# LN0 and adaLN stage: no low parts on GpSimd, and some w_ada blocks multiplied as plain fp32 between and after LN0's transposes

## The chip, the cores and the metric

The kernel runs on one core of a Trainium2 chip. Its engines are named as in the profile: PE (TensorE matmul) and PEld (its weight load), DVE (VectorE), ACT (ScalarE), POOL (GpSimd) and SP (SyncE, which here only issues DMAs). The metric is the device time of one execution in microseconds (us).

## The reference, cut to what matters

One layer of an encoder trunk over 512 prompt rows and 64 sample rows of width 2048, in float32. The stage in question computes the first modulated input u and the first products with w_in:

```python
mod = (jax.nn.silu(c) @ w_ada + b_ada).reshape(B, 6, 1, D_MODEL)
sh1, sc1, g1, sh2, sc2, g2 = (mod[:, i] for i in range(6))
u = ln_plain(x) * (1 + sc1) + sh1
mix, k_new, v_new, pool_new = token_mixer(u, ...)      # begins with u @ w_in
```

`ln_plain` is a layer norm without parameters, c is one row for the prompt and one for the sample, w_ada is 2048 x 12288. Only sh1 and sc1 (columns 0 to 4095, 33.6 MB) belong to this stage; the other four are computed on DVE during attention.

## The kernel before

Matmuls are made in two or three fp32r products: a matrix is split into a high part (`hi`, an fp32r copy by ACT) and a low part (`lo`, the float32 value minus `hi`). The helper `Weights` does it for streamed weights: SP loads a block of 512 KB into a slot (L174), `advance` lets ACT write `hi` (L202) and then DVE or POOL write `lo` (L207). `take` hands PE the pair of a block and keeps three blocks split ahead. A slot is free for the next load when `lo` is written.

The stage in program order, which each engine follows strictly:

- x arrives in five tiles of 128 tokens (the last has 64). `stats` computes mean and variance on DVE and centres the tile (L496 on DVE, for tiles 1 and 3 L494 on ACT). `xpose` transposes it on PE in four groups of four (L507), one PSUM bank `AT[b]` for each group, and ACT copies the banks to axt (L512). A small product (L514) and `rs_evac` spread 1/std over the partitions.
- Then 64 w_ada blocks, in eight groups of eight: the loop at L604. A block is 512 rows of 256 columns, and four blocks make 256 columns of sh1 or sc1. `c4` holds silu(c) as high and low parts in four columns, so L613 and L614 are eight matmuls of 256 columns a block: `c4` times `hi`, `c4` times `lo`. The blocks alternate between DVE and POOL for their low part: `(None, nc.gpsimd) * 4` at L451.
- In group i also, for the 256 columns of group i - 1: `arow_copy` (DVE, after block 1), `ada_minis` (PE L550 and DVE L555, after block 3), and in blocks 4 to 7 `make_u`, which scales x (L566, DVE), and writes u's high part (L574, ACT) and low part (L581, DVE) for its two rows of 128 features, `a` and `b`.
- From group 2 on, after each block one program step `prog(i - 2, c, k)`: six matmuls (L299, L301, L303) of q, k, v and one gate for head 0, four columns of tiles c and two feature rows k. The steps of blocks 1, 3, 5 and 7 need feature row `b` of the group before.
- After blocks 3 and 7: `split_w`, w_in's rows split by ACT (L114) and DVE (L115), and `load_w`, their next load on SP (L463).

A tail finishes the program steps of groups 6 and 7; then attention of head 0 starts, with products from `q.take()` (the tile name `hi` at L299).

Of the kernel before, what the change touches and what calls it, by code (L numbers as in the profile page):

```python
# [14 lines left out]
P = 128  # L15
# [17 lines left out]
def split3(ap, a):  # L33
    return ap.rearrange("p (a b) -> p a b", a=a)
# [3 lines left out]
def tile_trunk(ctx, tc, x_prompt, x_sample, c_prompt, c_sample, cache_k, cache_v, state_pool,  # L38
# [3 lines left out]
    nc = tc.nc  # L42
# [58 lines left out]
    c4 = region("to", [P, 256], F32R)  # L101
# [11 lines left out]
    def split(hi, lo, src, eng=None):  # L113
        nc.scalar.activation(hi, src, AF.Copy)  # L114
        (eng or nc.vector).tensor_tensor(lo, src, f(hi), op=OP.subtract)  # L115
# [27 lines left out]
    class Weights:  # L143


        def __init__(self, slots, pairs, engs=(None,)):
            self.free, self.pairs, self.engs, self.late = list(slots), pairs, engs, False
            self.items, self.uses, self.at, self.units, self.sums = [], [], [], [], []
            self.nl = self.nu = self.ns = 0
            self.ready, self.sum_of = [], {}  # L150

        def load_item(self, ap):
            self.items.append(ap)
# [15 lines left out]
            return split3(self.at[i][:, :kk * n], kk)  # L169

        def load(self):
            while self.nl < len(self.items) and self.free:
                self.at[self.nl] = self.free.pop(0)
                nc.sync.dma_start(self.view(self.nl), self.items[self.nl])  # L174
                self.nl += 1

# [17 lines left out]
        def advance(self, late=False):  # L194
            if self.nu < len(self.units):
                i = self.nu
                self.nu += 1
                a, b, _ = self.units[i]
                raw = self.view(a) if b is None else self.sum_of.pop(i)
                kk, n = raw.shape[1], raw.shape[1] * raw.shape[2]  # L200
                hi, lo = (split3(t[:, :n], kk) for t in self.pairs[i % len(self.pairs)])
                nc.scalar.activation(hi, raw, AF.Copy)  # L202
                self.combine(i + 1)

                def low():
                    eng = nc.gpsimd if fill.bg and fill.bg[0][0] == "mod" else self.engs[i % len(self.engs)]
                    (eng or nc.vector).tensor_tensor(lo, raw, f(hi), op=OP.subtract)  # L207
                    if b is None:
                        self.release(a)

                if late:
                    fill.at(3, low)
                else:
                    low()
                self.ready.append((hi, lo))
# [209 lines left out]
    t1 = cv(128)  # L425
    cv.o = 1536
    t3, t2 = cv(1024), cv(128)
    e4 = small[:, 44:46]
    cv.o = 1536
    ut = [cv(576), cv(576)]  # L430
# [5 lines left out]
    for i in range(4):  # L436
# [5 lines left out]
    nc.scalar.dma_start(t3[0:15, :], state_pool[0, 0])  # L442

    nc.gpsimd.memset(zz, 0.0)
    make_identity(nc, ident)
    nc.gpsimd.memset(nhalf, -0.5)
    nc.gpsimd.iota(icnt, pattern=[[1, 15]], base=1, channel_multiplier=0, allow_small_or_imprecise_dtypes=True)
    nc.vector.reciprocal(icnt, icnt)

    halves = [t[:, o:o + 1024] for t in (RAW[0], RAW[1], RAW[2], xt2[:, 2048:4096]) for o in (0, 1024)]  # L450
    q0 = Weights(halves, PAIRS,  # L451
                 (None, nc.gpsimd) * 4)
    for i in range(8):
        for part in range(2):
            for kb in range(4):
# [15 lines left out]
    csv = split3(csil, 2)  # L471
    nc.scalar.activation(c4[:, 64:192], zz, AF.Copy)
    split(c4v[:, 0:2, :], c4v[:, 2:4, :], csv)
    nc.vector.tensor_tensor(e4[0:4, :], ident[0:4, 0:2], ident[0:4, 2:4], op=OP.add)

    axt0 = region("oa", [P, KT, 320])
# [7 lines left out]
    def stats(i):  # L484
        n = ntok[i]
        m = mvs[i % 3][0:n]
        xt = xtok[i][0:n]
        for s in range(4):
            nc.vector.bn_stats(st6[0:n, s, :], xt[:, s * 512:s * 512 + 512])
        nc.vector.bn_aggr(m[:, 0:2], st6[0:n])  # L490
        if i in (1, 3):
            neg = small[0:n, 56 + i:57 + i]
            nc.vector.tensor_scalar(neg, m[:, 0:1], -1.0, None, op0=OP.mult)
            nc.scalar.activation(xt, xt, AF.Identity, bias=neg)  # L494
        else:
            nc.vector.tensor_scalar(xt, xt, m[:, 0:1], None, op0=OP.subtract)  # L496
        nc.vector.tensor_scalar_add(m[:, 2:3], m[:, 1:2], EPS)
        nc.gpsimd.tensor_tensor(m[:, 3:4], m[:, 2:3], nhalf[0:n], op=OP.pow)

    def xpose(i):  # L500
        n = ntok[i]
        t0 = 128 * i if i < 4 else TP
        for b in range(4):
            p = AT[b]
            for jj in range(4):
                j = 4 * b + jj
                nc.tensor.transpose(p[:, jj * n:jj * n + n], xtok[i][0:n, j * P:j * P + P], ident[0:n, 0:n])  # L507
            pv = split3(p[:, 0:4 * n], 4)
            for hf in range(2):
                a, e = max(t0, HOFF[hf]), min(t0 + n, HOFF[hf] + HS[hf])  # L510
                if a < e:
                    nc.scalar.activation(axt(hf, 4 * b, 4, a - HOFF[hf], e - HOFF[hf]), pv[:, :, a - t0:e - t0],  # L512
                                         AF.Copy, scale=ALPHA)
        nc.tensor.matmul(MM[i % 2][:, 192:192 + n], mvs[i % 3][0:n, 3:4].to_broadcast([n, P]), ident[0:n, 0:n],  # L514
                         start=True, stop=True)

    def rs_evac(i):
        n = ntok[i]
        t0 = 128 * i if i < 4 else TP
        nc.vector.tensor_scalar(rs_r[:, t0:t0 + n], MM[i % 2][:, 192:192 + n], 1.0 / ALPHA, None, op0=OP.mult)  # L520
# [8 lines left out]
        nc.tensor.transpose(AT[3][:, 256 + 15 * c:271 + 15 * c], t3[0:15, c * P:c * P + P], ident[0:15, 0:15])  # L529
    nc.vector.tensor_copy(stT.rearrange("p a b -> p (a b)"), AT[3][:, 256:376])  # L530
    stats(1)
    for i in range(5):
        xpose(i)
        if i < 3:
            stats(i + 2)
        if i == 2:
            q0.advance()
        if i == 3:
            q0.advance()
        rs_evac(i)  # L540
    PS0 = [(MM[0][:, 192:512], MM[0][:, 512:768]), (MM[1][:, 192:512], MM[0][:, 768:1024]),
           (AT[0][:, 0:320], MM[1][:, 512:768]), (AT[1][:, 0:320], MM[1][:, 768:1024])]
    SEG = [[(0, 320, 0)], [(0, 192, 0), (192, 256, 1)]]
# [14 lines left out]
    def make_u(i):  # L558
        pieces = []

        def scale(j):
            t = ut[j % 2]
            for hf in range(2):
                for a, e, v in SEG[hf]:
                    o = HOFF[hf]
                    nc.vector.scalar_tensor_tensor(t[:, o + a:o + e], axt(hf, j, 1, a, e)[:, 0, :], shsc[:, 1, j, v:v + 1],  # L566
                                                   rs_r[:, o + a:o + e], op0=OP.mult, op1=OP.mult)

        def high(j):
            t = ut[j % 2]  # L570
            for hf in range(2):
                for a, e, v in SEG[hf]:
                    o = HOFF[hf]
                    nc.scalar.activation(xh(hf, j)[:, a:e], t[:, o + a:o + e], AF.Identity, bias=shsc[:, 0, j, v:v + 1])  # L574

        def low(j):
            t = ut[j % 2]
            for hf in range(2):
                for a, e, v in SEG[hf]:
                    o = HOFF[hf]  # L580
                    nc.vector.scalar_tensor_tensor(xl(hf, j)[:, a:e], t[:, o + a:o + e], shsc[:, 0, j, v:v + 1],  # L581
                                                   f(xh(hf, j)[:, a:e]), op0=OP.add, op1=OP.subtract)

        if i == 0:
            new_xh()
            new_xl()
        a, b = 2 * i, 2 * i + 1
        return [[(scale, a)], [(high, a), (scale, b)], [(low, a), (high, b)], [(low, b)]]
# [12 lines left out]
        nc.vector.tensor_copy(arow[0:4, :], AT[2 + i % 2][0:4, :])  # L601

    PROG = [(c, k) for c in range(4) for k in range(2)]
    for i in range(8):  # L604
        ps = AT[2 + i % 2]
        u = make_u(i - 1) if i else []
        for b in range(8):
            wh, wl = q0.take()
            part, kb = divmod(b, 4)
            for k in range(4):  # L610
                kk = kb * 4 + k
                o = ps[:, part * 256:part * 256 + 256]
                nc.tensor.matmul(o, c4[:, 4 * kk:4 * kk + P], wh[:, k, :], start=kk == 0, stop=False)  # L613
                nc.tensor.matmul(o, c4[:, 4 * kk:4 * kk + P], wl[:, k, :], start=False, stop=kk == 15)  # L614
            if i:
                if b == 1:
                    arow_copy(i - 1)
                if b == 3:
                    ada_minis(i - 1)
                if b >= 4:  # L620
                    for fn, j in u[b - 4]:
                        fn(j)
            if i >= 2:
                prog(i - 2, *PROG[b])
            if b in (3, 7):
                part = b // 4
                if i:
                    split_w(part)
                if i < 7:
                    load_w(i, part)  # L630
            if i == 7:
                if b == 1:
                    q.load()
                if b == 3:
                    load_w(7, 0)
                if b == 7:
                    load_w(7, 1)
# [925 lines left out]
```

## Time and profile before

| | |
|---|---|
| median of three runs | 3105.9 us (3105.35 to 3106.19) |
| the profiled execution | 3106.03 us, span 3104.3 us |
| PE, DVE, ACT, POOL busy over the span | 95%, 71%, 36%, 19% |
| mean granted clock of TensorE | 0.975 |
| the stage: start to the first matmul of attention | 0 to 220.35 us |
| repeating groups 2 to 7 | about 24 us each |

The page's busy shares are averages over the whole span. In its 40 slices of 77.6 us the first three, which hold this stage, show PE busy 6, 7 and 8 tenths, where most later slices show 9. A matmul's duration in a timeline is longer than the time until the next one starts, since they are pipelined; the pace is read from start to start. An fp32 matmul that is not a transpose stands as two records.

### The profile page before, as it was taken

The numbers are of one execution on the slowest core, as the hardware profiler recorded it, in microseconds if no ns is written. First come the engines' busy times: TensorE is split into PE (matmuls) and PEld (weight loads), VectorE is DVE, ScalarE is ACT, GpSimd is POOL, SyncE is SP. The second block draws the span as 40 slices with busy tenths as digits, with TensorE's granted clock in tenths as the row PEclk, the third lists the DMA queues.
The fourth block names the chain that finished last, engine by engine and source line by source line (L and its number), as shares of the span: only waits on it lengthen the run. The fifth ranks groups of instructions, "written<-read, shape, count | busy, mean of one in ns | idle before, by whom it ended". The sixth has DMA issues, their size and how long they took to land. (4 is left out here: it accounts for less than half of the span.)

```text
span 3104.3 us, 52673 instructions
## 1 busy us (share of the span) xinstructions
PE 2960.5 (95%) x21675; PEld 2909.0 (94%) x21675; DVE 2214.5 (71%) x3285; ACT 1132.4 (36%) x1536; POOL 593.8 (19%) x551
## 2 busy tenths in 40 slices
PE   6789999999999999998989899999999999999997
PEld 5788988899999999998879899999999999999997
DVE  7777666679887985688787877777777763333457
ACT  5442322334222223355643434443333432121333
POOL 4433232312332322044442000000000020000001
PEclk8899999999999999999989999999999999999998
DMA  8656444467554654755544434334343473333444
GB/s 272 201 155 202 141 129 137 138 197 214 161 168 143 180 157 117 215 155 171 151 142 129 117 97 113 105 105 113 98 120 95 123 256 116 101 101 116 146 155 152
DMA packets 636015, 458.13 MB, mean 148 GB/s; under 512 B 17215, under 2 KB 619807, under 8 KB 634430
## 3 DMA queue, kind: packets, MB, share of 16 engines
q1 hardware_dynamic: 621136, 406.38, 44.4%
q0 software_dynamic: 14336, 48.24, 4.4%
q8 instruction: 169, 2.77, 0.4%
q14 instruction: 72, 0.59, 0.1%
q10 hardware_dynamic: 302, 0.15, 0.0%
HBM read 422.66 MB, written 32.04 MB: 146 GB/s over the span
## 5 line engine op out<-in xcount | busy, mean ns | idle before, releaser
L202 ACT ACTIVATE hi<-raw 128x1024 fp32r<-128x1024 f32 x704 | 740.2, 1057 | 1120.2 <-PE bank L301 343.2
L207 DVE TENSOR_TENSOR lo<-raw,hi 128x1024 fp32r<-128x1024 f32 x668 | 841.6, 1262 | 414.6 <-ACT hi L202 407.9
L303 PE MATMUL mm<-xh,lo 128*128 128x320 f32 (+1 forms) x2912 | 713.4, 298 | 23.7 <-DVE lo L207 13.4
L299 PE MATMUL mm<-xh,hi 128*128 128x320 f32 (+1 forms) x2912 | 730.8, 304 | 0.9 <-ACT hi L202 0.9
L301 PE MATMUL mm<-xl,hi 128*128 128x320 f32 (+1 forms) x2912 | 712.6, 297 | 7.9 <-DVE xl L1096 7.9
L303 PEld LDWEIGHTS mm<-xh,lo 128*128 128x128 f32 x2912 | 487.9, 191 | 27.3 <-DVE lo L207 15.9
L299 PEld LDWEIGHTS mm<-xh,hi 128*128 128x128 f32 x2912 | 492.3, 191 | 11.1 <-issue 4.0
L301 PEld LDWEIGHTS mm<-xl,hi 128*128 128x128 f32 x2912 | 489.0, 191 | 13.1 <-DVE xl L1096 12.6
L357 DVE SCALAR_TENSOR_TENSOR late<-raw,csil,late 128x256 f32<-128x256 f32 x960 | 425.9, 503 | 13.2 <-DMA raw<-in_w_ada_dram 13.0
L1327 PE MATMUL bank<-xh,hi 128*128 128x288 f32 x1152 | 341.3, 296 | 3.5 <-ACT xh L1177 3.5
L1327 PE MATMUL bank<-xl,hi 128*128 128x288 f32 x1152 | 341.2, 296 | 1.6 <-DVE xl L1181 1.6
L1327 PE MATMUL bank<-xh,lo 128*128 128x288 f32 x1152 | 341.0, 296 | 1.6 <-DVE lo L207 1.6
L299 PE MATMUL bank<-xh,hi 128*128 128x320 f32 (+1 forms) x1280 | 315.9, 295 | 2.2 <-DVE misc L1283 2.2
L303 PE MATMUL bank<-xh,lo 128*128 128x320 f32 (+1 forms) x1280 | 314.3, 294 | 1.1 <-DVE lo L207 1.1
L301 PE MATMUL bank<-xl,hi 128*128 128x320 f32 (+1 forms) x1280 | 314.3, 294 | 0.0
L1327 PEld LDWEIGHTS bank<-xh,hi 128*128 128x128 f32 x1152 | 216.8, 188 | 3.7 <-ACT xh L1177 3.7
L1327 PEld LDWEIGHTS bank<-xl,hi 128*128 128x128 f32 x1152 | 216.7, 188 | 2.2 <-DVE xl L1181 2.2
L1327 PEld LDWEIGHTS bank<-xh,lo 128*128 128x128 f32 x1152 | 216.8, 188 | 1.9 <-DVE lo L207 1.9
L299 PEld LDWEIGHTS bank<-xh,hi 128*128 128x128 f32 x1280 | 213.9, 188 | 2.5 <-DVE misc L1283 2.5
L303 PEld LDWEIGHTS bank<-xh,lo 128*128 128x128 f32 x1280 | 213.7, 188 | 1.4 <-DVE lo L207 1.4
L301 PEld LDWEIGHTS bank<-xl,hi 128*128 128x128 f32 x1280 | 214.1, 188 | 0.0
L362 POOL PARTITION_ALL_REDUCE late<-late x32 | 117.7, 3679 | 279.8 <-DVE late L357 202.7
(399 smaller groups left out, 4385.2 us busy)
## 6 DMA issues: line engine op xcount, KB each, us to landing
raw<-in_w_ada_dram SPq DMA_DIRECT2D x176, 512.0 KB, 4.7
raw<-in_w_in_dram SPq DMA_DIRECT2D x120, 512.0 KB, 4.5
raw<-in_w_down_dram SPq DMA_DIRECT2D x120, 512.0 KB, 3.3
raw<-in_w_gate_dram SPq DMA_DIRECT2D x104, 512.0 KB, 4.3
raw<-in_w_up_dram SPq DMA_DIRECT2D x104, 512.0 KB, 5.1
raw<-in_w_out_dram SPq DMA_DIRECT2D x64, 512.0 KB, 4.5
raw<-in_w_sb_out_dram SPq DMA_DIRECT2D x32, 512.0 KB, 5.0
hd<-misc POOLq DMA_DIRECT2D x36, 288.0 KB, 2.4
```

What stands on the lines that cost most here:

```text
L202: nc.scalar.activation(hi, raw, AF.Copy)
L207: (eng or nc.vector).tensor_tensor(lo, raw, f(hi), op=OP.subtract)
L299: nc.tensor.matmul(o, wh[:, k, cw], xh(xk + k), start=s and u not in join, stop=False)
L301: nc.tensor.matmul(o, wh[:, k, cw], xl(xk + k), start=False, stop=False)
L303: nc.tensor.matmul(o, wl[:, k, cw], xh(xk + k), start=False, stop=e and u not in hold)
L357: nc.vector.scalar_tensor_tensor(acc[:, v, :], raw[:, k, :], s, acc[:, v, :], op0=OP.mult, op1=OP.add)
L362: nc.gpsimd.partition_all_reduce(late["red"], late["acc"][grp % 2], P, bass_isa.ReduceOp.add)
L1327: nc.tensor.matmul(b[BANK[m]], n[w][:, k, :], SOP[m][x](k), start=not st and k == 0 and i == 0, stop=k == 7 and i == 2, skip_group_check=st)
```

## The change

Three edits in one stage.

1. `q0`, the stream of w_ada, no longer names POOL: every low part is on DVE (or not made).
2. The units in `q0.direct` are multiplied as plain fp32: `advance` makes no high and low part for them, PE reads the raw block with `c4f`, a float32 copy of silu(c) (four matmuls of 256 columns, each two records, instead of eight), and the slot becomes free when these are done. `q0.ring` makes the slots of the stream a strict ring: block n + 8 goes where block n was, and loads stay in order.
3. The blocks of group 0, all direct, stand between the transposes, two after each of tiles 1 to 4, into the bank AT[2]; the transposes rotate over AT[0], AT[1] and AT[3]. `load_w(0, ...)` moves there too, and near the end `q.load()` moves from block 1 to block 3 of group 7.

```diff
-    q0 = Weights(halves, PAIRS,
-                 (None, nc.gpsimd) * 4)
+    q0 = Weights(halves, PAIRS)
+    q0.ring = halves
+    q0.direct = {u for u in range(64) if u < 8 or u % 8 in (2, 6) or u < 16 and u % 2 == 0}
...
         def load(self):
-            while self.nl < len(self.items) and self.free:
-                self.at[self.nl] = self.free.pop(0)
+            while self.nl < len(self.items):
+                if self.ring:
+                    n = len(self.ring)
+                    if self.nl >= n and self.uses[self.nl - n]:
+                        return
+                    self.at[self.nl] = self.ring[self.nl % n]
...
                 raw = self.view(a) if b is None else self.sum_of.pop(i)
+                if i in self.direct:
+                    self.ready.append((raw, a))
+                    return
...
-            p = AT[b]
+            p = AT[(0, 1, 3)[(4 * i + b) % 3]]
...
+    def ada_unit(ps, b):
+        blk = q0.take()
+        part, kb = divmod(b, 4)
+        o = ps[:, part * 256:part * 256 + 256]
+        for k in range(4):
+            kk = kb * 4 + k
+            if len(blk[0].shape) == 3 and isinstance(blk[1], int):
+                nc.tensor.matmul(o, c4f[:, 4 * kk:4 * kk + P], blk[0][:, k, :], start=kk == 0, stop=kk == 15)
+            else:
+                nc.tensor.matmul(o, c4[:, 4 * kk:4 * kk + P], blk[0][:, k, :], start=kk == 0, stop=False)
+                nc.tensor.matmul(o, c4[:, 4 * kk:4 * kk + P], blk[1][:, k, :], start=False, stop=kk == 15)
+        if isinstance(blk[1], int):
+            q0.release(blk[1])
+
     for i in range(5):
         xpose(i)
         if i < 3:
             stats(i + 2)
-        if i == 2:
-            q0.advance()
-        if i == 3:
-            q0.advance()
         rs_evac(i)
+        if i:
+            ada_unit(AT[2], 2 * i - 2)
+            ada_unit(AT[2], 2 * i - 1)
+            if i % 2 == 0:
+                load_w(0, i // 2 - 1)
...
-    for i in range(8):
+    for i in range(1, 8):
         ps = AT[2 + i % 2]
...
             if i == 7:
-                if b == 1:
+                if b == 3:
                     q.load()
-                if b == 3:
                     load_w(7, 0)
```

PE in LN0, before: from the second transposed tile on. The names at_74 to at_77 are the banks AT[0] to AT[3], xh holds the tiles of x, mm is where the small product goes.

```order
L507 MATMUL at_74<-ident,xh 128x128 x4
L507 MATMUL at_75<-ident,xh 128x128 x4
L507 MATMUL at_76<-ident,xh 128x128 x4
L507 MATMUL at_77<-ident,xh 128x128 x4
L514 MATMUL mm_73<-ident,small 128x128
L507 MATMUL at_74<-ident,xh 128x128 x4
```

The same place after the change; misc holds `c4f`, raw_65 is the first raw tile, which holds two blocks.

```order
L524 MATMUL at_74<-ident,xh 128x128 x4
L531 MATMUL mm_72<-ident,small 128x128
L524 MATMUL at_75<-ident,xh 128x128 x4
L524 MATMUL at_77<-ident,xh 128x128 x4
L524 MATMUL at_74<-ident,xh 128x128 x4
L524 MATMUL at_75<-ident,xh 128x128 x4
L531 MATMUL mm_73<-ident,small 128x128
L557 MATMUL at_76<-raw_65,misc 128x256 x8
L524 MATMUL at_77<-ident,xh 128x128 x4
```

The first tile's fourth group of transposes now writes the bank of its first, and two direct blocks stand between tile 1 and tile 2.

DVE in a repeating group, before: from the small bias step to the end of u's low part, feature row `a`. Here lo_70 and lo_71 are the low tiles of the weights, late holds the split w_in, misc the scaled x, oa and ob the transposed x, xl u's low part.

```order
L555 SCALAR_TENSOR_TENSOR misc<-at_77,vt_85 128x4 x2
L115 TENSOR_TENSOR late<-oc,late 128x512
L566 SCALAR_TENSOR_TENSOR misc<-oa,misc 128x320
L566 SCALAR_TENSOR_TENSOR misc<-ob_132,misc 128x192
L566 SCALAR_TENSOR_TENSOR misc<-ob_132,misc 128x64
L207 TENSOR_TENSOR lo_70<-raw_65,hi_68 128x1024
...
L581 SCALAR_TENSOR_TENSOR xl<-misc,xh 128x320
```

The same place after the change.

```order
L588 SCALAR_TENSOR_TENSOR misc<-at_77,vt_85 128x4 x2
L115 TENSOR_TENSOR late<-oc,late 128x512
L220 TENSOR_TENSOR lo_70<-oc,hi_68 128x1024
L599 SCALAR_TENSOR_TENSOR misc<-oa,misc 128x320
L599 SCALAR_TENSOR_TENSOR misc<-ob_134,misc 128x192
L599 SCALAR_TENSOR_TENSOR misc<-ob_134,misc 128x64
L220 TENSOR_TENSOR lo_71<-raw_65,hi_69 128x1024
...
L220 TENSOR_TENSOR lo_71<-raw_65,hi_69 128x1024
L614 SCALAR_TENSOR_TENSOR xl<-misc,xh 128x320
```

DVE has three low parts between L115 and u's last low part where it had two. POOL's queue before, from LN0's last small step on:

```order
L498 TENSOR_TENSOR small<-small 64x1
L207 TENSOR_TENSOR lo_70<-raw_65,hi_68 128x1024
L207 TENSOR_TENSOR lo_71<-raw_66,hi_69 128x1024
L207 TENSOR_TENSOR lo_70<-raw_67,hi_68 128x1024
L207 TENSOR_TENSOR lo_71<-oc,hi_69 128x1024
...
```

And after the change:

```order
L515 TENSOR_TENSOR small<-small 64x1
L693 MEMSET to 128x128
L694 AFFINE_SELECT to<-to 128x128
L713 MEMSET oc 128x64
L714 MEMSET oc 128x64
```

The 32 subtractions are gone from POOL, and its next work is attention's constants.

## Rows read from the trace of the kernel before

**Rows 1.** timeline of PE (start, us, engine, line, operation, tiles; idle before, releaser)

```profile
71.99 0.58 PE L301 MATMUL mm<-xl,late 128*128 128x256 f32 x1 [3.28 <-DVE xl L581]
...
125.56 1.05 PE L550 MATMUL at<-small,misc 4*128 4x2 f32 x8
...
126.53 0.53 PE L299 MATMUL mm<-xh,late 128*128 128x320 f32 x2
...
127.44 0.28 PE L613 MATMUL at<-hi,to 128*128 128x256 f32 x1
...
128.39 0.31 PE L299 MATMUL at<-xh,late 128*128 128x320 f32 x1
...
134.41 0.28 PE L613 MATMUL at<-hi,to 128*128 128x256 f32 x1
...
191.77 0.58 PE L301 MATMUL mm<-xl,late 128*128 128x256 f32 x1 [4.30 <-DVE xl L581]
...
206.13 0.43 PE L299 MATMUL mm<-xh,late 128*128 128x320 f32 x2
...
220.35 0.43 PE L299 MATMUL mm<-xh,hi 128*128 128x320 f32 x2
```

**Rows 2.** windows: length, PE, PEld, DVE, ACT, POOL, clock, DMA share, GB/s

```profile
119.87:143.81 23.94, 18.47 (x120) 17.40 (x120) 19.26 (x23) 11.27 (x16) 9.82 (x4) 0.86 0.63 198
```

**Rows 3.** waits from 33 to 200 us (total, times, longest)

```profile
PE mm L301 <- DVE xl L581: 32.3, 17, 4.3
```

**Rows 4.** timeline of ACT, the same group

```profile
127.38 0.63 ACT L114 ACTIVATE late<-oc 128x512 fp32r<-128x512 f32 x1 [3.72 <-PE mm L301]
```

**Rows 5.** timeline of DVE, the same group

```profile
128.04 0.69 DVE L115 TENSOR_TENSOR late<-oc,late 128x512 fp32r<-128x512 f32 x1 [1.17 <-ACT late L114]
...
128.65 0.55 DVE L566 SCALAR_TENSOR_TENSOR misc<-oa,misc 128x320 f32<-128x320 f32 x1
...
129.11 2.76 DVE L566 SCALAR_TENSOR_TENSOR misc<-ob,misc 128x192 f32<-128x192 f32 x2
...
131.79 1.21 DVE L207 TENSOR_TENSOR lo<-raw,hi 128x1024 fp32r<-128x1024 f32 x1
...
138.63 5.25 DVE L581 SCALAR_TENSOR_TENSOR xl<-misc,xh 128x320 fp32r<-128x320 f32 x3
```

**Rows 6.** timeline of POOL, the same group, first and last of three

```profile
129.03 2.42 POOL L207 TENSOR_TENSOR lo<-oc,hi 128x1024 fp32r<-128x1024 f32 x1 [9.16 <-ACT hi L202]
...
139.01 4.80 POOL L207 TENSOR_TENSOR lo<-raw,hi 128x1024 fp32r<-128x1024 f32 x2 [2.96 <-ACT hi L202]
```

**Rows 7.** timeline of DVE in the tail, POOL idle

```profile
203.97 0.60 DVE L566 SCALAR_TENSOR_TENSOR misc<-ob,misc 128x192 f32<-128x192 f32 x2
...
204.50 2.16 DVE L581 SCALAR_TENSOR_TENSOR xl<-misc,xh 128x320 fp32r<-128x320 f32 x6
```

**Rows 8.** timeline of PE in attention, fp32 products

```profile
264.52 2.32 PE L782 MATMUL at<-oc,misc 128*128 128x512 f32 x8
...
266.68 0.33 PE L784 MATMUL at<-oc,misc 128*128 128x64 f32 x2
```

**Rows 9.** windows, columns as in rows 2

```profile
30.00:40.00 10.00, 8.50 (x49) 7.96 (x50) 6.06 (x7) 8.74 (x14) 6.62 (x3) 0.66 0.52 158
...
40.00:60.00 20.00, 14.85 (x109) 13.18 (x107) 20.00 (x13) 11.49 (x13) 18.39 (x6) 1.00 1.03 330
```

**Rows 10.** timeline of ACT in LN0

```profile
17.47 2.00 ACT L494 ACTIVATE xh<-xh,small 128x2048 f32<-128x2048 f32 x1 [8.79 <-DVE small L493]
...
19.38 3.23 ACT L512 ACTIVATE oa<-at 128x512 f32<-128x512 f32 x6
```

**Rows 11.** timeline of PE in LN0, transposes

```profile
14.19 3.67 PE L507 MATMUL at<-ident,xh 128*128 128x128 f32 x16
...
23.34 1.91 PE L507 MATMUL at<-ident,xh 128*128 128x128 f32 x16
```

**Rows 12.** DMA from the start to 30 us, total

```profile
DMA packets 5164, 9.06 MB, mean 302 GB/s; under 512 B 311, under 2 KB 4573, under 8 KB 4588
```

More of the change, by code (lines that the diff above doesn't have):

```diff
@@ L149, in __init__ @@
             self.nl = self.nu = self.ns = 0
-            self.ready, self.sum_of = [], {}
+            self.ring = None
+            self.ready, self.sum_of, self.direct, self.np = [], {}, (), 0
         def load_item(self, ap):
@@ L171, in load @@
         def load(self):
-            while self.nl < len(self.items) and self.free:
-                self.at[self.nl] = self.free.pop(0)
+            while self.nl < len(self.items):
[4 more added lines that the diff above has]
+                    self.at[self.nl] = self.ring[self.nl % n]
+                elif self.free:
+                    self.at[self.nl] = self.free.pop(0)
+                else:
+                    return
                 nc.sync.dma_start(self.view(self.nl), self.items[self.nl])
@@ L199, in advance @@
                 raw = self.view(a) if b is None else self.sum_of.pop(i)
+                if i in self.direct:
+                    self.ready.append((raw, a))
+                    return
                 kk, n = raw.shape[1], raw.shape[1] * raw.shape[2]
-                hi, lo = (split3(t[:, :n], kk) for t in self.pairs[i % len(self.pairs)])
+                hi, lo = (split3(t[:, :n], kk) for t in self.pairs[self.np % len(self.pairs)])
+                self.np += 1
                 nc.scalar.activation(hi, raw, AF.Copy)
@@ L427, in tile_trunk @@
     t3, t2 = cv(1024), cv(128)
+    c4f = cv(192)
     e4 = small[:, 44:46]
@@ L444, in tile_trunk @@
     nc.gpsimd.memset(zz, 0.0)
+    nc.gpsimd.memset(c4f, 0.0)
     make_identity(nc, ident)
@@ L473, in tile_trunk @@
     split(c4v[:, 0:2, :], c4v[:, 2:4, :], csv)
+    nc.vector.tensor_copy(c4f[:, 0:64].rearrange("p (k f) -> p f k", f=4)[:, 0:2, :], csv)
     nc.vector.tensor_tensor(e4[0:4, :], ident[0:4, 0:2], ident[0:4, 2:4], op=OP.add)
@@ L531, in tile_trunk @@
     stats(1)
+    def ada_unit(ps, b):
[6 more added lines that the diff above has]
+                nc.tensor.matmul(o, c4f[:, 4 * kk:4 * kk + P], blk[0][:, k, :], start=kk == 0, stop=kk == 15)
+            else:
+                nc.tensor.matmul(o, c4[:, 4 * kk:4 * kk + P], blk[0][:, k, :], start=kk == 0, stop=False)
+                nc.tensor.matmul(o, c4[:, 4 * kk:4 * kk + P], blk[1][:, k, :], start=False, stop=kk == 15)
+        if isinstance(blk[1], int):
+            q0.release(blk[1])
     for i in range(5):
@@ L603, in tile_trunk @@
     PROG = [(c, k) for c in range(4) for k in range(2)]
-    for i in range(8):
+    for i in range(1, 8):
         ps = AT[2 + i % 2]
-        u = make_u(i - 1) if i else []
+        u = make_u(i - 1)
         for b in range(8):
[L608 to L615, printed above, removed]
-                if b == 1:
-                    arow_copy(i - 1)
-                if b == 3:
[L619 to L622, printed above, removed]
+            ada_unit(ps, b)
+            if b == 1:
+                arow_copy(i - 1)
+            if b == 3:
+                ada_minis(i - 1)
+            if b >= 4:
+                for fn, j in u[b - 4]:
+                    fn(j)
             if i >= 2:
@@ L626, in tile_trunk @@
                 part = b // 4
-                if i:
-                    split_w(part)
+                split_w(part)
                 if i < 7:
@@ L631, in tile_trunk @@
             if i == 7:
-                if b == 1:
+                if b == 3:
                     q.load()
-                if b == 3:
                     load_w(7, 0)
```

## The prediction

> **What bounds the kernel now.** I read the page first, then the stage by stretches, the waits, and the timelines of DVE, POOL and PE over one group. A group is eight w_ada blocks, the unit of the loop at L604. The part that the change touches lasts from the start to 220.35 us, where the first matmul of the attention stage runs [rows 1]. Groups 2 to 7 repeat: the restart of PE in group 2 is at 71.99 us, in group 7 at 191.77 us [rows 1], so a group takes (191.77 - 71.99) / 5 = 23.96 us. In one of them no engine is full: PE is busy 18.47 us, DVE 19.26, ACT 11.27, POOL 9.82, the DMA share is 0.63, the granted clock 0.86 [rows 2]. So a loop of waits sets the length. The waits name it: PE (L301) waits for the low part of u that DVE writes (L581), 4.3 us at the longest [rows 3], and ACT (L114) waits for PE (L301), 3.72 us in this group [rows 4]. That is one ring: PE's program step at block 3, ACT and DVE split w_in (L114, L115), DVE scales, splits and finishes u, PE's program step at block 1 of the next group restarts, and reaches block 3 again.
>
> The DVE half of the ring starts at 128.04 us and ends at 138.63 + 5.25 = 143.88 us: 15.84 us with hardly a gap [rows 5]. The reader is to see that three steps in it are slow while POOL works: POOL computes low parts in three rows from 129.03 to 139.01 us, the last with two of them [rows 6], and in just these stretches a pair of DVE scalings takes 2.76 us (twice) and the last three subtractions 5.25 us [rows 5]. The same pair with POOL idle takes 0.60 us, six subtractions 2.16 us [rows 7]. The loss is 2 x 2.16 + 5.25 - 1.08 = 8.5 us a group.
>
> **GpSimd's low parts go.** All 32 POOL subtractions are removed, so DVE runs at its undisturbed pace. Of 64 blocks 24 are direct by the set in the diff (8 in group 0, 4 in group 1, 2 in each later group; not 26), so DVE keeps 40 low parts, 6 in a later group where it had 4. The DVE half after: L115 0.69, three low parts at 1.21, two scalings of 0.55 + 0.60, two subtraction triples of 1.08 [rows 5, 7]: 0.69 + 3.63 + 2.30 + 2.16 = 8.8 us, where 15.84 stood. With ACT's 0.63 us ahead [rows 4] it is 9.4 us. All DVE work of a group, with three more low parts, the other L115 and about 0.9 for the row copy and bias, is 8.8 + 3.6 + 0.7 + 0.9 = 14.0 us.
>
> **Direct blocks on PE.** A split block is eight matmuls. Four blocks with their program steps run from 127.44 to 134.41 us at the full clock: 6.97 us, so 1.743 us for a block and a step, of which the block is 0.95 us (127.44 to 128.39) [rows 1]. A direct block is four fp32 matmuls of 256 columns. The nearest row is attention's fp32 product, which has different weights each time as well: four matmuls of 512, 384, 256 and 128 columns take 266.68 - 264.52 = 2.16 us, 1.69 ns a column [rows 8]. So 256 columns cost 0.432 us, a direct block 1.73 us, 0.78 more than a split one. Bounds: 0.95 from below (no dearer than a split block), and 3.46 from above (the same columns at half the clock). I take 1.73, since that row has the same type and a warm array.
>
> PE's group after: 8 x 1.743 + 2 x 0.78 + 0.97 for the small products (125.56 to 126.53 [rows 1]) = 16.47 us. The ring after: ACT's and DVE's 9.4 us, then PE from the step of block 1 to that of block 3 (5.6 us with one direct block and the small products) = 15.0 us. PE's sum is the larger, so PE itself becomes the bound at 16.5 us a group, and no wait of 4.3 us is left to lower its clock. DVE has 2.5 us to spare, the ring 1.5.
>
> **DMA.** A group moves eight blocks of 0.524 MB and 0.524 MB of w_in: 4.72 MB. The rate under full load is 330 GB/s (DMA share 1.03 [rows 9]), so 14.3 us, hidden behind 16.5 with 2 us over. New is that a direct block holds its slot until PE is done with it, and the ring loads in order, so on SP's queue the three loads behind it and a w_in load wait for PE too. A load has at least a group's length from there to its use, less the three units of lookahead, so I cost this at nothing; the cover is PE's 16.5 us, and the second rival prices its loss.
>
> **LN0.** The first eight blocks now run between the transposes, and the transposes have three banks where they had four. With three, the fourth group of x0's transposes needs the first bank again, whose evacuation stands behind ACT's centring of x1 (17.47 us; evacuations from 19.38 us, under 0.6 each [rows 10]). PE therefore waits until about 20.0 us with everything behind it, and finishes x1's transposes by 25.3 us (0.22 us each at the slow pace of 14.19 us [rows 11]) instead of 23.3. ACT's x2 to x4 evacuations are not late for it. Then four pairs of direct blocks (3.46 us each) alternate with transposes of x2, x3 and x4 (1.9 us by the row of x2 [rows 11], up to 2.3 with waits for ACT, 1.5 for x4 as it has half the columns) and their small product (0.25): PE is through at 45.3 us. The w_ada blocks are no wait: 9.06 MB had moved by 30 us, which is x and all eight blocks [rows 12]. Group 1 (4 direct, 4 split, 0.97 of small products) puts the small products' end at 51.6, and DVE's half (9.0 with the bias step; ACT's part lies earlier here) ends at 60.6 (its first triple at 59.5); PE does the other half of the group and the first block of group 2 by 57.9, then waits for the first low part of u until 59.5. Restart of group 2's second step: 61.4 us, where it was 71.99. Gain 10.6 us.
>
> **The sum.** Gain to group 2: 10.6. Five groups: 5 x (23.96 - 16.47) = 37.5. From group 7's restart to the end before: 220.35 - 191.77 = 28.58 us; after, 13.4 (rest of PE's group) + 14.2 (the same tail, 206.13 to 220.35 [rows 1]) = 27.6: gain 1.0. Together 49.1 us. I take off 2.5 us for one stretch at the low clock: after a thin second half of LN0 the granted clock was 0.66 from 30 to 40 us [rows 9], and the early wait for u in group 2 could bring such a stretch back. The profiled execution took 3106.0 us (span 3104.3), the median of the runs is 3105.9, so both stand for each other: 3106.0 - 46.6 = 3059.4, forecast 3059 us. The later stages keep their instructions; they only start earlier.
>
> **A rule against the change.** Attention's fp32 product costs 1.69 ns a column [rows 8], the split blocks' fp32r 0.95 us / 2048 columns = 0.46 ns [rows 1]: an fp32 column costs 3.6 of them, so no weight load stands open between the fp32 matmuls of that row. The Trainium skill, "TensorE: Matmul & The Clock Gate", section "Weight-path perf modes — Fast Weight Load (FWL) and DoubleRow", says that the fast weight load is on only where the type is not FP32; its section "LDWEIGHTS (loading the stationary operand)" gives 107 ns for 128 columns; by that page 24 direct blocks with eight open loads each would cost 21 us more (an estimate). By the row they are hidden, and the forecast goes by the row.
>
> **The rivals.**
> First, PE's clock stays low in LN0 and falls again in the groups. For: before, 0.66 of full clock at 30 to 40 us [rows 9], and a group averages 0.86 [rows 2]. Against: PE has no wait of several us left, and in LN0 the pace had doubled from x0's transposes to x2's by 23.34 us [rows 11]. Price: eight direct blocks at double time, 8 x 1.73 = 13.8, and one 5 us stretch at half pace in two or three groups, 2.5 each: 19 to 21 us, 3079 us.
>
> Second, transfers set the group. Half a group's loads (four blocks, one w_in pair: 2.36 MB) start when PE frees a direct slot: 7.15 us at 330 GB/s, and about 2 us until the first bytes; 9.2 us against PE's half of 8.24. If each burst had to land before the next, a group takes 18.3: six groups, 11 us, 3070 us. Against: the next burst's issue waits for PE, not for the landing.
>
> Third, slower: fp32 matmuls in between keep PE at 1.2 GHz for the whole stage. Place: all groups; price: group 2's restart near 90 (+18), five groups of 32.9 (+45), the tail 55 instead of 28.6 (+26): 3195 us. It turns the sign once a third of PE's 146 us in the stage runs at half pace (49 / 146). Against: attention's fp32 products stand among full-clock rows [rows 8].
>
> Fourth, the change doesn't do what it says: DVE's pace is not POOL's doing. Then groups gain only the lead of group 0: 10 us, 3096 us. Against: each slow DVE row lies on a POOL row [rows 5, 6].
>
> Fifth, the weight loads of direct blocks stand open, two a matmul. A load that nothing covers costs 0.97 / 8 = 0.12 us in the small products [rows 1], so a direct block costs 0.97 us more and 24 of them 23 us: 3082 us. Against: the 1.69 ns a column above, at 128 to 512 columns.
>
> **Chances.** Forecast (3053 to 3066) 0.67; second rival 0.12; first 0.11; fifth 0.04; fourth 0.03; third and other losses 0.03. The range 3052 to 3080 leaves out under 2 in 10: its low end is all the full clock and a restart 5 us earlier, its high end the first rival. A measurement of this kernel can tell 0.2%, 6.2 us: faster 0.95, within 0.02, slower 0.03.
>
> **What would show it.** Right: no POOL row before about 150 us besides the small powers; pairs of 64- and 192-column scalings at 0.60 us; direct blocks 1.73 us apart; restarts of the second program step 16.5 us apart from 61 us on; granted clock near 1.0; the attention stage's first matmul near 173 us. Wrong: a PE wait for w_ada or for a DVE low part in every group (the DVE row then sets 17 to 18 us), direct blocks at 3.5 us, or an attention stage that starts early and whose length grows.

## The result, and the profile after

The changed kernel takes 3056.17 us (median of four runs, 3054.38 to 3059.53), the kernel before beside it 3105.62 us (3098.75 to 3106.19). The ratio is 0.9846, with a 95% interval of 0.9835 to 0.9858: faster by 49.5 us. The forecast was 3059 us, from 3052 to 3080. The profiled execution after took 3059.53 us, span 3057.5.

The stage that is changed now ends at 170.28 us, where it ended at 220.35 [rows 1]; 50.1 us are won there. In the first fence are rows of PE's timeline: start, us, engine, line, operation, tiles.

```profile
23.74 3.62 PE L557 MATMUL at<-raw,misc 128*128 128x256 f32 x16
27.20 2.00 PE L524 MATMUL at<-ident,xh 128*128 128x128 f32 x16
...
48.81 1.05 PE L583 MATMUL at<-small,misc 4*128 4x2 f32 x8
...
58.86 0.43 PE L314 MATMUL mm<-xl,late 128*128 128x320 f32 x2
...
68.33 1.89 PE L557 MATMUL at<-oc,misc 128*128 128x256 f32 x8
69.86 0.50 PE L312 MATMUL at<-xh,late 128*128 128x320 f32 x1
...
70.85 0.28 PE L559 MATMUL at<-hi,to 128*128 128x256 f32 x1
...
170.28 0.43 PE L312 MATMUL mm<-xh,hi 128*128 128x320 f32 x2
```

The small products of group 1 end at 49.8 us and the second program step of group 2 is restarted at 58.86, where [rows 1] had 71.99. A direct block and its step last from 68.33 to 70.85, 2.52 us; a split block with its step took 1.743 [rows 1]. So a direct block costs 0.78 us more, as worked out.

The next fence is DVE's timeline in the same stretch of a group as [rows 5].

```profile
82.12 0.69 DVE L115 TENSOR_TENSOR late<-oc,late 128x512 fp32r<-128x512 f32 x1 [1.17 <-ACT late L114]
83.07 1.23 DVE L220 TENSOR_TENSOR lo<-oc,hi 128x1024 fp32r<-128x1024 f32 x1 [0.26 <-ACT hi L215]
84.21 0.55 DVE L599 SCALAR_TENSOR_TENSOR misc<-oa,misc 128x320 f32<-128x320 f32 x1
84.67 0.61 DVE L599 SCALAR_TENSOR_TENSOR misc<-ob,misc 128x192 f32<-128x192 f32 x2
...
88.46 2.06 DVE L614 SCALAR_TENSOR_TENSOR xl<-misc,xh 128x320 fp32r<-128x320 f32 x6
...
98.81 0.69 DVE L115 TENSOR_TENSOR late<-oc,late 128x512 fp32r<-128x512 f32 x1 [1.17 <-ACT late L114]
```

The pair of scalings is at 0.61 us, where [rows 5] had 2.76, and the six subtractions at 2.06. DVE's half of the ring lasts from 82.12 to 90.52, 8.4 us instead of 15.84. The same step comes again at 98.81: a group takes 16.69 us, it was 23.96. The window of one such group (length; busy time of PE, PEld, DVE, ACT and POOL; clock, DMA share, GB/s), which answers to [rows 2], and two of the waits from 33 to 160 us (who waited for whom: total, times, longest):

```profile
97.41:114.10 16.69, 16.69 (x121) 16.12 (x122) 12.97 (x24) 9.26 (x14) 0.00 (x0) 1.00 0.89 278
```

```profile
ACT late L114 <- PE mm L314: 36.1, 11, 5.5
DVE misc L588 <- PE at L583: 17.8, 8, 4.5
```

PE is busy for the whole group at the full clock, and the waits have turned round: ACT and DVE wait for PE. PE's wait for DVE of [rows 3], 32.3 us, is gone; of waits for u's low part, 0.6 us of PEld's are left between 33 and 160 us.

### The profile page after: what moved, and what is told of

It reads as the page before. It is cut to its first block, busy times and chain, and to the rows that moved or that the text cites. A ratio compares the mean times of both kernels' runs of the same rounds, so it can differ in the third digit from the quotient of the medians.

```text
span 3057.5 us, 52572 instructions
## 1 busy us (share of the span) xinstructions
PE 2951.5 (97%) x21675; PEld 2902.7 (95%) x21675; DVE 2159.0 (71%) x3294; ACT 1108.8 (36%) x1512; POOL 508.1 (17%) x520
## 5 line engine op out<-in xcount | busy, mean ns | idle before, releaser
L220 DVE TENSOR_TENSOR lo<-raw,hi 128x1024 fp32r<-128x1024 f32 x677 | 850.3, 1258 | 411.7 <-ACT hi L215 400.9
L215 ACT ACTIVATE hi<-raw 128x1024 fp32r<-128x1024 f32 x689 | 724.9, 1057 | 1126.1 <-PE bank L1351 390.9
L316 PE MATMUL mm<-xh,lo 128*128 128x320 f32 (+1 forms) x2912 | 713.7, 298 | 22.9 <-DVE lo L220 13.1
L314 PE MATMUL mm<-xl,hi 128*128 128x320 f32 (+1 forms) x2912 | 712.6, 297 | 7.9 <-DVE xl L1120 7.9
L314 PEld LDWEIGHTS mm<-xl,hi 128*128 128x128 f32 x2912 | 489.1, 191 | 13.1 <-DVE xl L1120 12.6
L314 PE MATMUL bank<-xl,hi 128*128 128x320 f32 (+1 forms) x1280 | 314.0, 294 | 0.0
L314 PEld LDWEIGHTS bank<-xl,hi 128*128 128x128 f32 x1280 | 213.7, 188 | 0.0
```

The lines of the kernel that those rows point to most:

```text
L314: nc.tensor.matmul(o, wh[:, k, cw], xl(xk + k), start=False, stop=False)
L316: nc.tensor.matmul(o, wl[:, k, cw], xh(xk + k), start=False, stop=e and u not in hold)
```

## The experiments

Below, a group's length is the distance between like DVE steps (L115) in the steady groups; the ratio is the median over that of the kernel before, timed beside it, with its interval.

| run | group, us | time, us | ratio (95%) |
|---|---|---|---|
| the kernel after | 16.69 | 3056.2 | 0.9846 (0.9835 to 0.9858) |
| dve_low | 15.53 | 3050.3 | 0.9819 (0.9805 to 0.9833) |
| direct_ln0_only | 15.53 | 3047.6 | 0.9810 (0.9796 to 0.9824) |
| direct_one | 15.91 | 3051.6 | 0.9818 (0.9805 to 0.9832) |
| direct_four | 18.26 | 3063.1 | 0.9870 (0.9855 to 0.9886) |
| ln0_only | 23.85 | 3102.2 | 0.9984 (0.9975 to 0.9993) |
| ln0_split | 16.69 | 3056.3 | 0.9843 (0.9829 to 0.9856) |
| pool_back | 17.42 | 3062.8 | 0.9863 (0.9847 to 0.9880) |
| pool_even | 22.4 | 3093.2 | 0.9967 (0.9955 to 0.9980) |
| pool_private | | 3138.8 | 1.0108 (1.0093 to 1.0123) |
| pool_set | 16.69 | 3056.7 | 0.9844 (0.9830 to 0.9859) |
| row_on_act | 15.33 | 3047.3 | 0.9815 (0.9800 to 0.9830) |
| best | 15.34 | 3051.1 | 0.9826 (0.9812 to 0.9839) |

### GpSimd's low parts alone, and all but them

dve_low is the kernel before with one line changed:

```
-    q0 = Weights(halves, PAIRS,
-                 (None, nc.gpsimd) * 4)
+    q0 = Weights(halves, PAIRS)
```

> The kernel before, with all low parts on DVE; no block is direct and LN0 keeps its order. Theory A (GpSimd's subtractions slow DVE's steps in the ring): the pair of scalings falls from 2.76 to 0.60 us and the last triple from 5.25 to about 1.1, although DVE now has eight low parts a group instead of four. A group then costs the larger of PE's sum (16.69 - 2 x 0.78 = 15.1 us) and DVE's work (12.97 + 2 x 1.21 = 15.4): 15.4 to 16.0 us where 23.96 stood; five groups give 40 to 43 us and the first ones about 4: 3058 to 3063 us. Theory B (the time came from the direct blocks, which take work from ACT and DVE): with more work on DVE than before the groups stay above 21 us and the time above 3090 us.

This one line wins 56 us, more than the whole change. A group takes 15.53 us. DVE, with eight low parts a group instead of four, is busy for 15.14 us of it, where it showed 19.26 with four [rows 2]:

```profile
96.75:112.28 15.53, 15.39 (x122) 14.98 (x121) 15.14 (x25) 11.16 (x17) 0.00 (x0) 1.00 0.98 305
```

ln0_only is the kernel after with GpSimd's low parts back and direct blocks in group 0 alone:

```
+    q0 = Weights(halves, PAIRS, (None, nc.gpsimd) * 4)
+    q0.direct = {u for u in range(64) if u < 8}
```

> The kernel after, but only the eight blocks of group 0 are direct (between LN0's transposes), and in groups 1 to 7 every second low part is GpSimd's again, as before. Theory A: the groups go back to about 24 us each, and only the lead of LN0 is left, about 10 to 12 us: 3094 to 3097 us. Theory B (the early blocks or the direct ones were what mattered): at least half of the 49 us stays, below 3080 us.

It keeps 4.4 us of the 49.5, less than either theory had (3102.2 us, where theory A had 3094 to 3097). Its groups are those of before.

### The direct blocks

direct_ln0_only has `u < 8` as the whole set of direct blocks, direct_one `u < 8 or u % 8 == 2 or u < 16 and u % 2 == 0`, direct_four `u < 8 or u % 2 == 0`; all else is the kernel after.

> The kernel after, with direct blocks in group 0 alone; groups 1 to 7 split all eight blocks, low parts on DVE. Theory A (PE's own sum bounds a group of the kernel after): PE's sum falls to 16.69 - 2 x 0.78 = 15.1 us, DVE's work rises to 12.97 + 2 x 1.21 = 15.4 us; a group takes 15.4 to 15.8 us, five of them 4.5 to 6.5 us less than after: 3049 to 3052 us. Theory B (the direct blocks are needed to relieve DVE): waits of PE for DVE come back and a group is 16.7 us or more: 3056 us or more.

> The kernel after, with one direct block in each of groups 2 to 7 instead of two (groups 0 and 1 as in the kernel after). Theory A: PE's sum is 16.69 - 0.78 = 15.9 us, DVE's work 14.2, so PE stays the bound at 15.9 us: 6 x 0.78 = 4 to 5 us less than after, 3051 to 3053 us, with PE without waits in the groups. Theory B: no less than after, since what is saved on PE returns as waits for DVE: 3055 to 3057 us.

> The kernel after, with four direct blocks in each of groups 2 to 7 instead of two. Theory A (PE's sum sets the group): 16.69 + 2 x 0.78 = 18.25 us a group, 6 x 1.56 = 9 us more than after, 3064 to 3067 us, with PE never waiting. Rival (a direct block's late slot release makes transfers late): waits of PE for w_ada and more than 19 us a group, 3070 us or more.

All three came out by theory A, with groups of 15.53, 15.91 and 18.26 us, as worked out; two times lay about 1 us below their ranges, direct_ln0_only at 3047.6 and direct_four at 3063.1. The windows of one group show PE filled in the last two (direct_one first, then direct_four):

```profile
97.54:113.45 15.91, 15.91 (x123) 15.55 (x122) 14.11 (x25) 10.21 (x16) 0.00 (x0) 1.00 0.95 300
```

```profile
102.04:120.30 18.26, 18.26 (x121) 17.27 (x120) 10.97 (x21) 7.24 (x13) 0.00 (x0) 1.00 0.83 260
```

So in the kernel after, where GpSimd no longer works, each direct block in the groups costs time: none of them, two, four make 15.53, 16.69, 18.26 us. In none of these runs do the transfers set the group, not even with four slots held until PE is done.

ln0_split instead splits the eight blocks between LN0's transposes; the direct ones in groups 1 to 7 stay:

```
+    q0.direct = {u for u in range(64) if u % 8 in (2, 6) and u > 15 or 7 < u < 16 and u % 2 == 0}
```

> The kernel after, but the eight blocks of group 0 are split (hi on ACT, low part on DVE) where they stand between LN0's transposes; the direct blocks of groups 1 to 7 stay. Theory A (the lead into group 2 comes from the freed DVE; the direct blocks of LN0 add little, as the two runs with all low parts on DVE in the groups reach group 2 at the same time with and without them): within 3 us of the kernel after, 3054 to 3059 us. Theory B (direct blocks in LN0 are worth the 10 us of the forecast): 3063 us or more.

3056.3 us, the same as the kernel after. dve_low and direct_ln0_only are the same comparison in the other groups: their step of group 1 (L115, after the small products) stands at 50.51 and 50.42 us, in the kernel before at 56.20. So once GpSimd's low parts are gone in groups 0 and 1 as well, the program is early in group 2 without the fp32 blocks and without their new place: the second program step's L301 stands at 59.29 us in dve_low, at 58.86 in the kernel after (its L314), at 71.99 in the kernel before. The fp32 blocks can bring most of this lead too. pool_back below keeps GpSimd's low parts in group 1 beside fp32 blocks in groups 0 and 1, and has the same step at 61.49 us; ln0_only, with fp32 blocks in group 0 alone, has it at 68.23. The strict ring, the three banks and the moved loads are not in dve_low either; no run moved them by themselves.

### What GpSimd does to DVE

pool_private is the kernel after and, from the end of LN0 on, subtractions that no one waits for, over a part of the tile of x4 that is not used any more:

```
+    pa, pb = xt2[:, 0:1024], xt2[:, 1024:2048]
+    nc.gpsimd.memset(xt2[:, 0:2048], 0.0)
+    for _ in range(45):
+        nc.gpsimd.tensor_tensor(pa, pa, pb, op=OP.subtract)
```

> The kernel after, and beside it GpSimd works from the end of LN0 on 45 subtractions of 1024 columns over a part of SBUF that nothing else uses in this stage: no instruction waits for them. Theory A (a lock for the whole instruction): each DVE step with two inputs in SBUF waits for one GpSimd subtraction of about 2.4 us to end, so a 64-column step takes about 2.4 us where it takes 0.27; DVE's 20 such steps of a group take over 40 us, so the 45 subtractions, done in 110 to 140 us, let only two or three groups through: 3120 to 3160 us. Theory B (what slowed DVE was waiting for GpSimd's results or for slots that it frees): no change, 3054 to 3060 us. Theory C (the two share the bandwidth): a 1024-column subtraction of DVE takes about twice its 1.21 us and a 64-column step about 0.5 us: some 30 us more, 3085 us.

The program is slower than the kernel before. GpSimd's row, and the groups of DVE's operations between 60 and 150 us (busy, mean ns of one; idle time before):

```profile
41.47 129.21 POOL L640 TENSOR_TENSOR oc<-oc 128x1024 f32<-128x1024 f32 x45
```

```profile
L599 DVE SCALAR_TENSOR_TENSOR misc<-ob,misc 128x192 f32<-128x192 f32 x4 | 10.0, 2504 | 0.0
L614 DVE SCALAR_TENSOR_TENSOR xl<-misc,xh 128x64 fp32r<-128x64 f32 x4 | 9.5, 2364 | 0.0
...
L634 DVE COPY misc<-at 4x512 f32<-4x512 f32 x2 | 1.3, 672 | 0.0
```

A step of 64 columns takes 2364 ns, one of 192 columns 2504: the 0.14 us between them is what they differ by when nothing disturbs them (0.27 and 0.41 us), and the 2.1 us on top are the rest of a GpSimd subtraction. Sharing of bandwidth would have scaled both.

The trace shows it step by step. Of the two-input steps of these four lines (L115, L220, L599, L614) 44 began while a subtraction ran, and all of one length end at the same distance behind that subtraction's end: 0.08 us for 64 columns, 0.21 for 192, 0.35 for 320, 0.55 for 512, 1.08 for 1024. The other 10 began 0.07 to 0.08 us ahead of a subtraction and kept their own length (the low part at 62.00 us its 1.21 us), and there the subtraction took longer: 3.37 us behind that low part, where the shortest of the 45 took 2.34. So whichever of the two begins second waits for the other's end. The copy out of PSUM keeps 672 ns, and the bias step (L588), one of whose two inputs is in PSUM, 146 ns (157 in pool_set below).

The lengths of 2504 and 2364 ns stand in the kernel before too, in the slow triple of [rows 5], whose two small subtractions each wait for one of GpSimd's pair:

```profile
L581 DVE SCALAR_TENSOR_TENSOR xl<-misc,xh 128x192 fp32r<-128x192 f32 x1 | 2.5, 2509 | 0.0
L581 DVE SCALAR_TENSOR_TENSOR xl<-misc,xh 128x64 fp32r<-128x64 f32 x1 | 2.4, 2355 | 0.0
```

pool_set puts 45 writes of zeros (not the 60 of the expectation) in the place of the subtractions:

```
+    for _ in range(45):
+        nc.gpsimd.memset(xt2[:, 0:2048], 0.0)
```

> The kernel after, and beside it GpSimd writes zeros into the same unused part of SBUF 60 times (2048 columns each) and reads nothing. Theory A in the form that GpSimd's reads are what holds DVE: DVE's steps keep 0.27, 0.41, 0.54 and 1.21 us and the time stays at 3054 to 3060 us. The form that any GpSimd work holds DVE: the 64-column step takes over 1 us and the time rises by tens of us. The Trainium skill, "SBUF — State Buffer", section "Who interferes with whom", has the first form: an instruction of DVE with two SBUF inputs contends with a GpSimd instruction that reads SBUF, not with one that only writes.

No change: GpSimd is busy for 84 us from 41.41 us on, and DVE's steps keep their lengths:

```profile
41.41 84.05 POOL L638 MEMSET oc<- 128x2048 f32 x45 [10.96 <-PE at L524]
```

```profile
L599 DVE SCALAR_TENSOR_TENSOR misc<-ob,misc 128x192 f32<-128x192 f32 x10 | 4.1, 411 | 0.0
...
L614 DVE SCALAR_TENSOR_TENSOR xl<-misc,xh 128x64 fp32r<-128x64 f32 x10 | 2.8, 277 | 0.0
```

So a GpSimd instruction that reads two SBUF inputs holds a DVE step with two SBUF inputs to its end, and one that only writes SBUF does not. The Trainium skill, "SBUF — State Buffer", section "Who interferes with whom", says that a DVE instruction with two SBUF inputs contends with a GpSimd instruction that reads SBUF, not with one that only writes it; both runs agree with it. A GpSimd instruction with one input was not tried.

### Where the held stretches fall

pool_back gives the odd split blocks' low parts of the kernel after back to GpSimd, `q0 = Weights(halves, PAIRS, (None, nc.gpsimd) * 4)`, with the direct blocks left as they are.

> The kernel after, with the low parts of the odd split blocks on GpSimd again (four a group, as before); direct blocks, ring and LN0 stay. Theory A (while GpSimd's subtraction runs, a DVE step with two inputs stands still until it ends): DVE's pairs and triples take about 2.7 and 5 us again, a group goes back to 23 to 25 us and the time to 3095 to 3106 us, though DVE has only two low parts of its own left. Theory B (fewer low parts relieve DVE): groups stay at 16.7 us, 3056 us.

Theory A missed this by over 30 us: with four GpSimd subtractions a group, as many as before, a group takes 17.42 us. DVE's and GpSimd's timelines of one group:

```profile
90.82 2.76 DVE L599 SCALAR_TENSOR_TENSOR misc<-ob,misc 128x192 f32<-128x192 f32 x2
93.50 2.05 DVE L614 SCALAR_TENSOR_TENSOR xl<-misc,xh 128x320 fp32r<-128x320 f32 x6
95.47 0.68 DVE L115 TENSOR_TENSOR late<-oc,late 128x512 fp32r<-128x512 f32 x1
96.41 3.06 DVE L220 TENSOR_TENSOR lo<-raw,hi 128x1024 fp32r<-128x1024 f32 x1 [0.26 <-ACT hi L215]
```

```profile
86.47 2.41 POOL L220 TENSOR_TENSOR lo<-oc,hi 128x1024 fp32r<-128x1024 f32 x1 [2.19 <-ACT hi L215]
90.86 2.63 POOL L220 TENSOR_TENSOR lo<-raw,hi 128x1024 fp32r<-128x1024 f32 x1 [1.98 <-ACT hi L215]
95.50 6.19 POOL L220 TENSOR_TENSOR lo<-raw,hi 128x1024 fp32r<-128x1024 f32 x2 [2.01 <-ACT hi L215]
```

The scalings are still held twice, but GpSimd's last two subtractions start at 95.50 us, when DVE has written u, and hold a low part that PE does not yet need. DVE's half is 10.1 us long (85.47 to 95.55) instead of 15.84, and PE is nearly full again (17.23 of 17.44 us).

GpSimd's pair does not come later than before: it starts 10.03 us behind DVE's L115 of the group, in the kernel before 10.97 us behind it (139.01 - 128.04 [rows 5, 6]). It is DVE that is through earlier. In the kernel before, one of DVE's own low parts and 0.37 us of waiting for ACT stand ahead of the last triple:

```profile
137.49 1.23 DVE L207 TENSOR_TENSOR lo<-raw,hi 128x1024 fp32r<-128x1024 f32 x1 [0.37 <-ACT hi L202]
```

In pool_back no low part stands there, since one of the blocks is direct, and so the six subtractions run through undisturbed just ahead of the pair. Of the 5.8 us that the half lost, 1.6 are this low part and its wait, and 4.2 the last triple (5.25 us, 1.06 undisturbed). That the place decides is tried once more in pool_even, the kernel before with the even blocks on GpSimd, `(nc.gpsimd, None) * 4`:

> The kernel before, with GpSimd taking the even blocks' low parts instead of the odd ones'; the same number of its subtractions, four a group. Theory A (what counts is on which DVE steps of the ring the held stretches fall): two of the four then fall outside DVE's half of the ring; the half takes 0.69 + 2 x 1.21 + 2.3 + 2.16 + 2 x 2.2 = 12.0 us instead of 15.84 and a group about 20.1: 3083 to 3092 us. Rival (the number of GpSimd's subtractions counts, wherever they fall): 23.9 us a group, 3102 to 3108 us.

A group takes 22.4 us (from 75.79 to 187.58 in five), 3093.2 us in all, so the number alone doesn't decide; but theory A, too, had forecast less, about 20.1 us a group and at most 3092 us. Its 12.0 us for DVE's half was too low: it is 14.4, because the pair of subtractions still falls on the triples, one GpSimd subtraction fewer in the scalings:

```profile
122.44 2.69 DVE L566 SCALAR_TENSOR_TENSOR misc<-oa,misc 128x320 f32<-128x320 f32 x1
125.06 0.60 DVE L566 SCALAR_TENSOR_TENSOR misc<-ob,misc 128x192 f32<-128x192 f32 x2
...
128.45 6.30 DVE L581 SCALAR_TENSOR_TENSOR xl<-misc,xh 128x320 fp32r<-128x320 f32 x6
```

Together with two runs from above and the kernel after, pool_back gives the two halves of the change by themselves, all with direct blocks between LN0's transposes:

| low parts of the odd blocks | no direct blocks in groups 1 to 7 | four in group 1, two in each of groups 2 to 7 |
|---|---|---|
| on GpSimd | 23.85 us a group, 3102.2 us | 17.42 us, 3062.8 us |
| on DVE | 15.53 us, 3047.6 us | 16.69 us, 3056.2 us |

Either half alone takes most of the loss away. Done together, the second has nothing left to take and only its price remains.

### Past the change

In dve_low DVE is busy for 15.14 us of 15.53. row_on_act takes the row copy off it:

```
-        nc.vector.tensor_copy(arow[0:4, :], AT[2 + i % 2][0:4, :])
+        nc.scalar.activation(arow[0:4, :], AT[2 + i % 2][0:4, :], AF.Copy)
```

> The kernel before with all low parts on DVE, as in the run of that kind, and the copy of the 4 x 512 row out of PSUM (0.67 us a group on DVE) moved to ACT. Theory A: there a group of 15.53 us has DVE busy 15.15 us and PE 15.4 with its short waits; without the copy DVE has 14.5 and PE's own sum of 15.1 bounds: 15.1 us a group, 2 to 3 us less than 3050, so 3047 to 3048 us. Rival: ACT's copy comes late for the small products and PE waits for it: 3050 to 3055 us.

best is direct_ln0_only with the same edit.

> The two edits that the runs point to together: low parts on DVE in groups 1 to 7 without direct blocks there, direct blocks in group 0 between LN0's transposes, and the 4 x 512 row copy on ACT. Theory A: groups of 15.3 us (PE's own sum, as in the run with the copy moved), and no gain from LN0's order: 3045 to 3048 us. Rival (with DVE relieved, LN0's order now shows): 3040 to 3044 us.

The window of a group of row_on_act, and of best over 16 us:

```profile
96.71:112.05 15.34, 15.34 (x123) 15.00 (x122) 14.57 (x25) 11.63 (x18) 0.00 (x0) 1.00 0.99 312
```

```profile
97.00:113.00 16.00, 16.00 (x127) 15.66 (x127) 14.97 (x26) 12.29 (x19) 0.00 (x0) 1.00 1.03 324
```

PE shows busy for all of row_on_act's 15.33 us, yet 0.2 us of them are a wait that the busy time hides. One pair of matmuls in the group is longer than the 0.43 us of its neighbours, and of PEld's waits between 65 and 145 us this one is left, once a group:

```profile
106.04 0.64 PE L301 MATMUL mm<-xl,late 128*128 128x320 f32 x2
```

```profile
PEld mm L301 <- DVE xl L580: 0.9, 5, 0.2
```

So PE still waits there for u's low part, and its own sum is about 15.1 us (16.69 - 2 x 0.78), as the expectation had it; the group did not come down to it. The 0.2 us a group that the edit brings over dve_low and direct_ln0_only is under what the times can tell: the four versions stand between 3047 and 3051 us, with overlapping intervals, and best, whose last split of w_in is the earliest of all (156.92 us), measured 3 us above direct_ln0_only (158.08) and above the 3045 to 3048 us that were expected. The medians of all four are 5 to 9 us below the kernel after; only best's interval overlaps with that of the kernel after.

## Why the prediction was right, point by point

- **GpSimd's low parts slow DVE's half of the ring.** Right, in mechanism and size: 8.4 us against the 8.8 worked out; DVE's work a group 12.97 us against 14.0. dve_low shows that it is enough by itself, and pool_private that no dependence is needed for it.
- **PE becomes the bound.** Right: 16.69 us against 16.47, PE busy throughout. The 0.78 us of a direct block holds: direct_one, the kernel after and direct_four lie 0.78 us a block apart (15.91, 16.69, 18.26). So the 0.22 us are in the rest of the sum, which is 16.69 - 2 x 0.78 = 15.13 us, not 8 x 1.743 + 0.97 = 14.91. About half of them stand in [rows 1]: the program step behind the small products lasts from 126.53 to 127.44, 0.91 us, where the sum has 0.79 (1.743 - 0.95).
- **Direct blocks on PE: 1.73 us, loads hidden.** Right: two of them last from 23.74 to 27.20, 1.73 us each. The fifth rival (24 x 0.97 us) is out. So is the estimate of 21 us that the prediction worked out from the Trainium skill, "TensorE: Matmul & The Clock Gate", section "LDWEIGHTS (loading the stationary operand)"; the measurement decides. What the prediction did not work out is the sum without them. It had all terms for it: PE 14.91 and DVE 14.0 + 2 x 1.21 = 16.4 for the same 16.5 us, so that the direct blocks gain nothing once GpSimd is idle. Measured, they cost 1.16 us a group.
- **LN0 and group 1: gain 10.6.** Measured 71.99 - 58.86 = 13.1 us; the terms are each 1 to 3 us early (LN0 through on PE at 43.4 against 45.3 us, small products 49.8 against 51.6, DVE's half 58.1 against 60.6). But its cause was not the new place of the blocks, which the prediction's words "the first eight blocks now run between the transposes" suggest: dve_low reaches group 2 within 0.5 us as early with the old order, ln0_split within 0.8 us with split blocks in the new place, and ln0_only with fp32 blocks there has only 4 us. What counts is that in group 1, too, either GpSimd's low parts go or some blocks are direct (pool_back). The fourth rival's price, "the lead of group 0: 10 us", was mis-sized for the same reason.
- **The term for a stretch at low clock: 2.5 us.** Did not come; the granted clock is 1.00 in every window from 23.7 us, where the direct blocks begin, to 171 us. Before the change it was 0.66 from 30 to 40 us [rows 9]. Now the low stretch stands earlier, with 0.74 from 13 to 20 us and 0.58 from 20 to 23.7. With that the first rival is out.
- **The sum.** Its parts came out at 13.1, 36.4 and 0.6 us (to group 2's restart, five groups, from group 7's restart at 142.29 us to the end) where 10.6, 37.5 and 1.0 were worked out: 50.1 us at the stage's end against 49.1 before the 2.5 us were taken off. That the total is within 1 us is partly luck: a gain 2.5 us too small in LN0 and group 1 stands against 1.5 us too much behind it.
- **Transfers hidden; second and third rival out.** PE waits for no block in the groups, at a DMA share of 0.8 to 1.1, and fp32 matmuls did not keep the clock down.
- **Later stages keep their length.** Within the scatter: 50.1 us of lead at the stage's end, 49.5 between the medians. In the profiled execution alone the lead is 46.8 us at the end of the span; the other runs of this kernel were 3 to 5 us shorter than that one, and where these few us lie was not followed up.

Left open: what the ring, the banks and the moved loads are worth each by itself.

## What to carry to other kernels

Before giving work to an idle GpSimd, look at what DVE does at that moment: a subtraction on GpSimd held DVE's two-input steps for 8.5 / 4 = 2.1 us on average, where DVE itself needs 1.21 us for it, so the help cost more than it saved. When a change has two halves that cure one wait, price each half without the other; here the second was a loss of 1.16 us a group, hidden in a gain of 49 us. A step's busy time in a profile can be another engine's: 8.5 of DVE's 19.26 us were waiting.

## What the runs showed of the hardware

A DVE step of 64 columns beside GpSimd's subtractions took 2364 ns and one of 192 columns 2504 ns, against 277 and 411 ns beside GpSimd's writes of zeros: the delay does not depend on the length of the DVE step. A DVE copy out of PSUM was not delayed (672 ns in both). A DVE step that begins ahead of the subtraction is not held, and the subtraction waits instead: in pool_private a subtraction took 2.34 to 3.37 us, 129.21 / 45 = 2.87 us from start to start. The eight fp32 matmuls of two direct blocks took the pace of attention's product from 23.74 us on, in LN0, with PE never idle between the transposes.
